# A hybrid decoder trunk: transposing attention weights, queries and keys by DMA, and using them one to two projection groups later

## The chip, the cores and the metric

The kernel runs on one core of a Trainium2 chip. The metric is the device time of one execution in microseconds (us). The engines are TensorE (PE in the profile; PEld is its weight load), VectorE (DVE), ScalarE (ACT), GpSimd (POOL) and SyncE (SP), which here only issues DMAs. Each engine takes its instructions in a fixed order, and an instruction that waits holds up all behind it on its engine.

## The reference, cut to what matters

Two layers (`DEPTH = 2`) over 512 tokens of width 2048. Each layer normalises its input, multiplies it by one wide matrix, feeds three groups of heads, and multiplies their concatenated outputs by a second matrix:

```
proj = rmsnorm(x) @ w_in                 # 512 x 7696
A: y_conv = B * conv3(C * h) * silu(g)   # 512 channels, causal, width 3
B: q, k = rmsnorm per head(q), (k)       # 8 heads of 128, blocks of 128 queries
   z = q k^T / sqrt(128), masked to k < q
   w = exp(log_sigmoid(z) + sum over later keys of log_sigmoid(-z))
   y_sb = (w v) * silu(g)
C: gated linear attention (GLA), 4 heads, chunks of 64, decay exp(cumsum(g))
x = x + concat(y_conv, y_sb, y_gla) @ w_out
```

Weights, inputs and outputs are float32. The kernel keeps that accuracy by splitting an operand into a high and a low fp16 half and adding three products (high x high, high x low, low x high).

## The kernel before, in words

**Projections.** The columns of both matrices are cut into groups of 256: 30 groups of `w_in` and 8 of `w_out` for each layer, 76 in all (`specs`, L261). A group's weights come in two halves of 1 MB. `fetch` (L292) loads a half through SP into a `st` tile (3 buffers); `wmax` (L306) squares it on ACT; `wscale` (L314) takes the maximum over partitions on POOL and makes a power of two on DVE; `whi` (L343, the ACT line is L348) writes the high half `wh`, `wlo` (L351, DVE line L355) the low half `wl` (3 buffers each). `weights` (L368) loads one group ahead. PE uses a group in one of three shapes: `project_cols` (L502, output channels on partitions), `project_toks` (L526, tokens on partitions) and `project_by_token` (L539). Two of the three PSUM banks of pool `psp` hold a group's result.

**Order within a layer.** The GLA inputs come first, then the GLA itself (L666 to L793), then half of the convolution (`conv_in`, `conv_out`), then four attention stages `j` (L856), each of two heads with the groups V, G (gate), Q and K; then the other half of the convolution, then the output projection, group by group (L973). The results of the branches go into the fp16 tiles `mh` and `ml` by `mixsplit` (L580): channel tile 0 to 3 for the convolution, 4 to 11 for attention, 12 to 15 for GLA.

**An attention stage.** V is split into `vh`, `vl`; G becomes the gate `g`. For Q and for K: the squares of each head's row are summed on ACT (L884), a reciprocal root is refined on DVE (`rsqrt`, L189), the rows are scaled into `raw` (L892), PE transposes its eight 128x128 tiles in float32 into PSUM (L900), and ACT and DVE split them into fp16 halves with the K gain as a scale for each partition (L901, L902). Then for each of the two heads and each of two chunks of query tiles (`CHUNKS`, tiles 3 and 2 together, 0 and 1 together): PE makes the scores (L912, L914), ACT and DVE turn them into weights (L918 to L932, with a reversed scan in L928), PE transposes the weights in float32 (L938: seven tiles for the first chunk, three for the second), ACT and DVE split them into `wh`, `wl` (L940, L941), PE multiplies them with V (L946), DVE applies the gate (L949) and `mixsplit` stores.

**What sets the order.** Instructions are emitted in program order and then arranged on each engine by a scheduler with its own timeline; loads of weights have high priority. Where PE's next projection group has room, the scheduler puts transposes, scores and products of attention between its matmuls. The start of the program, up to `order.__exit__` (L496), is written out by hand for DVE and ACT.

**GLA scratch.** The tiles `src16`, `tgt16`, `att16` and `attd` (L137 to L142) have buffers of their own, zeroed once at the start.

Of the kernel before, what the change touches and what calls it, by code (L numbers as in the profile page):

```python
# [5 lines left out]
F32 = mybir.dt.float32  # L6
F16 = mybir.dt.float16
# [10 lines left out]
P = 128  # L18
# [12 lines left out]
CHUNKS = ((((3, 0), (2, 512)), ((0, 0, 256), (1, 256, 256), (2, 512, 256), (3, 768, 128))),  # L31
          (((0, 0), (1, 128)), ((0, 0, 256), (1, 256, 128))))
# [3 lines left out]
def hybrid_trunk(ctx, tc, x, norm_g, w_in, conv_w, conv_b, sb_qn_g, sb_kn_g,  # L36
# [30 lines left out]
    def sm(n, tag, bufs=None):  # L67
        return small.tile([P, n], F32, tag=tag, name=nm(tag), bufs=bufs)
# [64 lines left out]
    avg = const.tile([P, P], F32, tag="avg", name="avg")  # L133
    G.memset(avg, 1.0 / P)
    wup = const.tile([16, depth, 256], F32, tag="wup", name="wup")

    attd = const.tile([P, NT, 2, P], F32, tag="attd", name="attd")  # L137
    att16 = [const.tile([P, NT, 2, P], F16, tag=f"att{i}", name=f"att{i}") for i in range(2)]

    HT = P // 2  # L140
    src16 = [[const.tile([P, seq], F16, tag=f"src{b}{i}", name=f"src{b}{i}") for i in range(2)] for b in range(2)]
    tgt16 = [[const.tile([P, NT, 2, HT], F16, tag=f"tgt{b}{i}", name=f"tgt{b}{i}") for i in range(2)] for b in range(2)]  # L142
    G.memset(attd, 0.0)
# [26 lines left out]
    rows.append((wup, gla_w_up.rearrange("l r c -> r l c")))  # L170
# [32 lines left out]
    kg = const.tile([P, depth], F32, tag="kg", name="kg")  # L203
# [39 lines left out]
    def layer_consts():  # L243
        pps = bank(psm, "m")
        T.transpose(pps[:, :NP], prow, ident[:NP, :NP])
        V.tensor_copy(par, pps[:, :NP])
        for l in range(depth):
            V.tensor_reduce(onmax[:, l:l + 1], pcol("on", l), AX.X, ALU.max, apply_absolute_value=True)
            V.tensor_scalar(onmax[:, l:l + 1], onmax[:, l:l + 1], float(P) ** 0.5, None, ALU.mult)

            gq = sm(2, "kg")
            V.scalar_tensor_tensor(gq[:, 0:1], pcol("qn", l), float(P) ** -0.5, pcol("kn", l), ALU.mult, ALU.mult)
            V.tensor_scalar(gq[:, 1:2], allmax(gq[:, 0:1], 1, "k"), 2.0 ** -20, None, ALU.max)
            pow2(zun[:, l:l + 1], gq[:, 1:2], -20.0, "k")
            V.tensor_scalar(nzun[:, l:l + 1], zun[:, l:l + 1], -1.0, None, ALU.mult)
            V.reciprocal(gq[:, 1:2], zun[:, l:l + 1])
            V.tensor_scalar(kg[:, l:l + 1], gq[:, 0:1], gq[:, 1:2], 2.0 ** -10, ALU.mult, ALU.mult)
            V.tensor_scalar(nbu[:, l, :], par[:, base["bu"] + 2 * l:base["bu"] + 2 * l + 2], -1.0, None, ALU.mult)
# [235 lines left out]
    for a in src16[0] + src16[1] + tgt16[0] + tgt16[1]:  # L494
        V.memset(a, 0.0)
    order.__exit__(None, None, None)  # L496

    for l in range(depth):
# [71 lines left out]
        mh, ml = mix  # L570
        pmix = sm(8, "pmix")
# [36 lines left out]
        V.tensor_scalar(gu[:, 1:2], u, 2.0 ** 35, None, ALU.mult)  # L608
        lrT = wk([LR, seq], "e")
        V.tensor_copy(lrT, tp[:LR, :])  # L610
        Pc = wk([P, 2, seq], "raw", 1)
        for p in range(2):
            gp = bank(psm, "m")
            T.matmul(gp, wup[:, l, p * P:(p + 1) * P], lrT, start=True, stop=True)
# [73 lines left out]
        for p in range(2):  # L688
            Pp, q_, k_ = Pc[:, p, :], gq[:, p, :], gk[:, p, :]

# [84 lines left out]
            for hh in range(2):  # L775
# [7 lines left out]
                T.matmul(ms, avg, sq, start=True, stop=True)  # L783
# [23 lines left out]
        def conv_in(j):  # L807
# [3 lines left out]
            for c in range(2):  # L811
                S.activation(hb[:, c, :], ps[c], AF.Copy, scale=u)
            ps, u = project_cols()
# [4 lines left out]
            for c in range(2):  # L818
# [6 lines left out]
                for d in (1, 2):  # L825
                    V.scalar_tensor_tensor(y[:, c, d:], uc[:, c, :seq - d], w_(2 - d), y[:, c, d:], ALU.mult, ALU.add)  # L826
            return y

        def conv_out(j, y):
# [9 lines left out]

            if j:  # L840
# [15 lines left out]
        for j in range(4):  # L856
# [12 lines left out]
            V.tensor_scalar(vu[:, 0:1], u, 2.0 ** 14, None, ALU.mult)  # L869
            V.tensor_scalar(vu[:, 1:2], u, 1.0, None, ALU.mult)  # L870
            ps, u = project_cols()
            g = gate(ps, u, bm[:, 1:2])
            gm = allmax(bm[:, 0:1], 1, "b")
            m = sm(1, "sbm")
            V.scalar_tensor_tensor(m, gm, vu[:, 0:1], bm[:, 1:2], ALU.mult, ALU.mult)
            s_ = mixscale(2 + j, m, "b")
            qkT = []
            for tag, gain in (("qT", 2.0 ** 10), ("kT", kg[:, l:l + 1])):
                ps, u = project_toks(xh, xl)
                sq = sm(8, "qs")  # L880
                for t in range(NT):
                    for hh in range(2):
                        o = (t % 2) * GW + hh * P
                        S.activation(junk(P), ps[t // 2][:, o:o + P], AF.Square, accum_out=sq[:, 2 * t + hh:2 * t + hh + 1])  # L884
# [5 lines left out]
                raw = wk([P, NT, GW], "raw", 1)  # L890
                for b in range(2):
                    V.tensor_tensor(raw[:, 2 * b:2 * b + 2, :].rearrange("p a (h c) -> p (a h) c", c=P),  # L892
                                    ps[b].rearrange("p (a c) -> p a c", c=P),
                                    rs[:, 4 * b:4 * b + 4].rearrange("p (a o) -> p a o", o=1).to_broadcast([P, 4, P]),
                                    ALU.mult)
                nT_ = wk([P, 2, 2, seq], tag, dt=F16)
                tp = bank2()
                for hh in range(2):
                    for t in range(NT):
                        T.transpose(tp[:, hh, t * P:(t + 1) * P], raw[:, t, hh * P:(hh + 1) * P], ident)  # L900
                S.activation(nT_[:, 0], tp, AF.Copy, scale=gain)  # L901
                V.scalar_tensor_tensor(nT_[:, 1], tp, gain, nT_[:, 0], ALU.mult, ALU.subtract)  # L902
                qkT.append(nT_)
            qT, kT = qkT
            for hh in range(2):
                for qtiles, regs in CHUNKS:
                    q0 = min(t for t, _ in qtiles)
                    zw = sum(n for _, _, n in regs)
                    z = bank2().rearrange("p a c -> p (a c)")
                    for t, o in qtiles:  # L910
                        for i, (a_, b_) in enumerate(((0, 0), (0, 1), (1, 0))):
                            T.matmul(z[:, o:o + (t + 1) * P], qT[:, a_, hh, tsl[t]], kT[:, b_, hh, :(t + 1) * P],  # L912
# [3 lines left out]
                    a = wk([P, zw], "za")  # L916
# [16 lines left out]
                    wT = bank2().rearrange("p a c -> p (a c)")  # L933
                    for kt, ko, n in regs:
                        for t, o in qtiles:
                            if t >= kt:
                                c0 = ko + n - (q0 + 2 - t) * P
                                T.transpose(wT[:, c0:c0 + P], w[:, o + kt * P:o + (kt + 1) * P], ident)  # L938
                    wh, wl = (wk([P, zw], "w" + c, 1, F16) for c in "hl")
                    S.activation(wh, wT[:, :zw], AF.Copy, scale=2.0 ** 14)  # L940
                    V.scalar_tensor_tensor(wl, wT[:, :zw], 2.0 ** 14, wh, ALU.mult, ALU.subtract)  # L941
                    op = bank(psm, "m")[:, :2 * P]
                    hs = slice(hh * P, (hh + 1) * P)
                    for i, (kt, ko, n) in enumerate(regs):
                        for a_, b_ in ((vh, wh), (vh, wl), (vl, wh)):
                            T.matmul(op[:, 2 * P - n:], a_[:, kt, hs], b_[:, ko:ko + n], start=i == 0 and b_ is wh and a_ is vh,  # L946
                                     stop=i == len(regs) - 1 and a_ is vl, skip_group_check=True)
                    y = wk([P, 2 * P], "e")
                    V.scalar_tensor_tensor(y, op, vu[:, 1:2], g[:, hh, q0 * P:(q0 + 2) * P], ALU.mult, ALU.mult)  # L949
                    mixsplit(4 + 2 * j + hh, y, s_, q0)  # L950

        conv_out(1, conv_in(1))
# [20 lines left out]
        for gi in range(NG):  # L973
# [9 lines left out]
            else:  # L983
                ps, u = project_toks(mh, ml, (2, 3) if gi < 2 else ())
# [31 lines left out]
```

## Time and profile before

| What | Value |
|---|---|
| median of 3 runs | 1809.04 us (1807.43 to 1809.38) |
| the profiled execution | 1814.08 us |
| its span, first to last instruction | 1812.3 us |
| granted TensorE clock, mean | 0.996 |
| DMA packets | 180859, 183.74 MB |

The span is that of the one execution from which every row below comes. In a row of grouped instructions, "x160" is their number, then come their busy time in us and the mean ns of one; after the second bar stands the time for which the engine was idle just before them, and what ended it. PE's matmuls overlap in their pipe, so that the time of one is longer than the distance between two. A row of a stretch ("369.80:464.40") gives each engine's busy time in it.

### The profile page before, as it was taken

The page shows a single profiled execution, that of the slowest core. Times are in us where ns is not written, and L with a number is a line of the kernel's source. Part 1 is how long each engine was busy: PE and PEld are TensorE (multiplying, and loading weights), DVE is VectorE, ACT ScalarE, POOL GpSimd, SP SyncE. Part 2 cuts the span into 40 slices and gives each one's busy share as a digit, 9 for nine tenths or more (in the row PEclk, how much of TensorE's full clock was granted, in tenths as well). Part 3 has the DMA queues.
Part 4 walks back from the last instruction along what each step waited for, and adds up shares of the span by engine and source line. Part 5 has one row for each costly group of instructions (what it writes and reads, how often), then busy time and mean ns, then how long its engine had stood idle before and what let it go on. Part 6 is the DMA issues. An engine that isn't in the chain of part 4 may idle for free. (4 is left out here: it accounts for less than half of the span.)

```text
span 1812.3 us, 31149 instructions
## 1 busy us (share of the span) xinstructions
PE 1776.2 (98%) x13164; PEld 1271.9 (70%) x13164; DVE 1046.3 (58%) x1949; ACT 1106.9 (61%) x1671; POOL 43.2 (2%) x98
## 2 busy tenths in 40 slices
PE   7999999999999999999999998999999999999999
PEld 5744456878778764688886454568696878547888
DVE  5456777647464747533464566875655657465432
ACT  8567575567576765555554675675767666665431
POOL 0000000000000000000000000000000000000000
PEclk9999999999999999999999999999999999999999
DMA  6322222232322323354423232222323222224441
GB/s 214 116 93 93 71 93 72 73 113 71 105 83 91 97 74 116 115 182 144 133 81 117 94 93 70 94 82 82 94 91 97 71 94 94 93 94 140 141 139 47
DMA packets 180859, 183.74 MB, mean 101 GB/s; under 512 B 7842, under 2 KB 179948, under 8 KB 180208
## 3 DMA queue, kind: packets, MB, share of 16 engines
q1 hardware_dynamic: 171712, 172.30, 30.2%
q10 hardware_dynamic: 9008, 9.45, 1.6%
q8 instruction: 103, 1.69, 0.4%
q14 instruction: 36, 0.29, 0.1%
HBM read 173.36 MB, written 8.39 MB: 100 GB/s over the span
## 5 line engine op out<-in xcount | busy, mean ns | idle before, releaser
L311 ACT ACTIVATE junk<-st 128x2048 uint8<-128x2048 f32 (+1 forms) x152 | 290.4, 1910 | 290.7 <-DMA st<-in_w_in_dram 203.0
L523 PE MATMUL psp<-wl,m 128*128 128x256 f16 x1664 | 453.5, 273 | 0.0
L522 PE MATMUL psp<-wh,m 128*128 128x256 f16 x1664 | 453.5, 273 | 0.0
L524 PE MATMUL psp<-wh,m 128*128 128x256 f16 x1664 | 453.0, 273 | 0.0
L355 DVE SCALAR_TENSOR_TENSOR wl<-st,ws,wh 128x2048 f16<-128x2048 f32 (+1 forms) x120 | 282.2, 2354 | 118.6 <-ACT wh L348 117.6
L348 ACT ACTIVATE wh<-st,ws 128x2048 f16<-128x2048 f32 (+1 forms) x120 | 239.4, 1996 | 64.1 <-PE psp L524 40.8
L522 PE MATMUL psp<-wh,x 128*128 128x256 f16 x768 | 209.3, 273 | 0.0
L523 PE MATMUL psp<-wl,x 128*128 128x256 f16 x768 | 209.3, 273 | 0.0
L524 PE MATMUL psp<-wh,x 128*128 128x256 f16 x768 | 208.8, 273 | 0.0
L514 PE MATMUL psp<-x,wh 128*128 128x512 f16 x512 | 194.9, 381 | 1.0 <-ACT qT L648 1.0
L515 PE MATMUL psp<-x,wh 128*128 128x512 f16 x512 | 194.8, 381 | 0.0
L516 PE MATMUL psp<-x,wl 128*128 128x512 f16 x512 | 194.4, 381 | 0.0
L514 PE MATMUL psp<-m,wh 128*128 128x512 f16 x512 | 194.1, 379 | 0.0
L515 PE MATMUL psp<-m,wh 128*128 128x512 f16 x512 | 194.0, 379 | 0.0
L516 PE MATMUL psp<-m,wl 128*128 128x512 f16 x512 | 193.2, 379 | 0.0
L516 PEld LDWEIGHTS <-wl 128*128 128x128 f16 x1024 | 100.3, 98 | 120.5 <-issue 4.7
L514 PEld LDWEIGHTS <-wh 128*128 128x128 f16 x1024 | 100.3, 98 | 118.7 <-issue 4.8
L515 PEld LDWEIGHTS <-wh 128*128 128x128 f16 x1024 | 100.4, 98 | 118.2 <-issue 5.6
L524 PEld LDWEIGHTS <-m 128*128 128x128 f16 x1664 | 162.8, 98 | 20.2 <-issue 1.7
L523 PEld LDWEIGHTS <-m 128*128 128x128 f16 x1664 | 162.9, 98 | 20.1 <-issue 1.0
L522 PEld LDWEIGHTS <-m 128*128 128x128 f16 x1664 | 162.9, 98 | 19.6 <-issue 0.3
L321 DVE TENSOR_SCALAR wq<-wgm 128x1 f32<-128x1 f32 x76 | 16.2, 213 | 250.3 <-POOL wgm L318 249.3
(270 smaller groups left out, 2425.9 us busy)
## 6 DMA issues: line engine op xcount, KB each, us to landing
st<-in_w_in_dram SPq DMA_DIRECT2D x120, 1024.0 KB, 5.3
st<-in_w_out_dram SPq DMA_DIRECT2D x32, 1024.0 KB, 5.8
x<-in_x_dram SPq DMA_DIRECT2D x4, 1024.0 KB
qT<-in_x_dram ACTq DMA_DIRECT2D x8, 512.0 KB, 4.0
qT<-xs ACTq DMA_DIRECT2D x8, 512.0 KB, 3.7
xs<-x SPq DMA_DIRECT2D x14, 256.0 KB, 2.5
out_dram<-kT SPq DMA_DIRECT2D x14, 256.0 KB, 2.1
g<-in_norm_g_dram ACTq DMA_DIRECT2D x2, 512.0 KB
```

The costliest lines, as they stand in the source:

```text
L311: S.activation(junk(HK * n).rearrange("p (k n) -> p k n", k=HK), staged[i][h][:, :, :n], AF.Square, accum_out=peak[i][:, h:h + 1])
L321: V.tensor_scalar(m, gm[:, 0:1], gm[:, 1:2], 2.0 ** -120, ALU.add, ALU.max)
L348: S.activation(wh[:, ks, :n], staged[i][h][:, ks, :n], AF.Copy, scale=s_)
L355: V.scalar_tensor_tensor(wl[:, ks, :n], staged[i][h][:, ks, :n], s_, wh[:, ks, :n], ALU.mult, ALU.subtract)
L514: T.matmul(o, wh[:, kk, cs], xh[:, :, k, :], start=st_, stop=False)
L515: T.matmul(o, wh[:, kk, cs], xl[:, :, k, :], start=False, stop=False)
L516: T.matmul(o, wl[:, kk, cs], xh[:, :, k, :], start=False, stop=en)
L522: T.matmul(o, ah[:, t, k, :], wh[:, kk, :n], start=st_, stop=False, skip_group_check=True)
L523: T.matmul(o, ah[:, t, k, :], wl[:, kk, :n], start=False, stop=False, skip_group_check=True)
L524: T.matmul(o, al[:, t, k, :], wh[:, kk, :n], start=False, stop=en, skip_group_check=True)
```

## The change

- `CHUNKS` keeps the places of the query tiles and drops the columns of the transposed weights.
- Q and K (L878 to L903): the square's output goes into `raw` and no longer into a scrap tile; `raw` for K is made by eight products of 128x128 that include the gain, now a full row `kg[:, l, :]` on all partitions (made once for each layer by one more matmul); ACT and DVE split `raw` from SBUF into a new tile `qp` (one buffer), and two DMAs from SP (`dma_start_transpose`, high and low) transpose its eight tiles into `qT` or `kT`.
- Attention weights: they are split before they are transposed, in the memory of `a`; four DMAs for each head (high and low of the two chunks) write the transposed tiles into a new tile `th`. PE's transposes in L900 and L938 are gone.
- Order: `attend` puts four closures into a list: the scores of head 0, of head 1, the products with V of head 0, of head 1. `go()` runs the next one. In the next stage the scores of head 0 come after group V, those of head 1 after G, the products of head 0 after Q and of head 1 after K; for the last stage the groups of the second convolution half stand in, and the products of head 1 come just before the output projection, whose first two groups take channel tile 11 late.
- GLA scratch: `src16` and `tgt16` are views of `mh`, `att16` of `ml`, in channel tiles 4 to 11, zeroed by POOL in each layer; `attd` is a work tile zeroed twice in each layer. The DVE memsets of the start are gone. `avg` is one column, read with a step of zero. The GLA up-projection `wup` is loaded by SP in each layer into a work tile.

The core of the diff:

```
-            for tag, gain in (("qT", 2.0 ** 10), ("kT", kg[:, l:l + 1])):
+            for gain in (None, kg[:, l, :]):
...
-                        S.activation(junk(P), ps[t // 2][:, o:o + P], AF.Square, accum_out=sq[:, 2 * t + hh:2 * t + hh + 1])
+                        S.activation(raw[:, t, hh * P:(hh + 1) * P], ps[t // 2][:, o:o + P], AF.Square,
+                                     accum_out=sq[:, 2 * t + hh:2 * t + hh + 1])
...
-                        T.transpose(tp[:, hh, t * P:(t + 1) * P], raw[:, t, hh * P:(hh + 1) * P], ident)
-                S.activation(nT_[:, 0], tp, AF.Copy, scale=gain)
-                V.scalar_tensor_tensor(nT_[:, 1], tp, gain, nT_[:, 0], ALU.mult, ALU.subtract)
+                            V.scalar_tensor_tensor(raw[:, t, hh * P:(hh + 1) * P], ps[t // 2][:, o:o + P],
+                                                   rs[:, 2 * t + hh:2 * t + hh + 1], gain, ALU.mult, ALU.mult)
...
+                parts = wk([P, 2, NT * GW], "qp", 1, F16)
+                S.activation(parts[:, 0], raw.rearrange("p t c -> p (t c)"), AF.Copy, scale=top)
+                V.scalar_tensor_tensor(parts[:, 1], raw.rearrange("p t c -> p (t c)"), top, parts[:, 0],
+                                       ALU.mult, ALU.subtract)
...
+                for i in range(2):
+                    nc.sync.dma_start_transpose(nT_[:, i].rearrange("p t h c -> p (t h) c"), parts[:, i])
...
-                                T.transpose(wT[:, c0:c0 + P], w[:, o + kt * P:o + (kt + 1) * P], ident)
-                    wh, wl = (wk([P, zw], "w" + c, 1, F16) for c in "hl")
-                    S.activation(wh, wT[:, :zw], AF.Copy, scale=2.0 ** 14)
-                    V.scalar_tensor_tensor(wl, wT[:, :zw], 2.0 ** 14, wh, ALU.mult, ALU.subtract)
+                    wh, wl = parts[:, :zw], parts[:, 896:896 + zw]
+                    S.activation(wh, w, AF.Copy, scale=2.0 ** 14)
+                    V.scalar_tensor_tensor(wl, w, 2.0 ** 14, wh, ALU.mult, ALU.subtract)
+                    for i, part in enumerate((wh, wl)):
+                        nc.sync.dma_start_transpose(th[hh][:, i, 7 * n:7 * n + zw // P, :], part)
...
+            later.extend((lambda: scores(0), lambda: scores(1), lambda: values(0), lambda: values(1)))
...
+            go()
...
-        conv_out(1, conv_in(1))
+        conv_out(1, conv_in(1, go), go)
+        while later:
+            go()
```

More of the change, by code (lines that the diff above doesn't have):

```diff
@@ L131, in make_masks @@
             V.tensor_scalar(masks[:, li, :], far, float(h), None, ALU.is_equal)
-    avg = const.tile([P, P], F32, tag="avg", name="avg")
+    avg = const.tile([P, 1], F32, tag="avg", name="avg")
     G.memset(avg, 1.0 / P)
-    wup = const.tile([16, depth, 256], F32, tag="wup", name="wup")
-    attd = const.tile([P, NT, 2, P], F32, tag="attd", name="attd")
-    att16 = [const.tile([P, NT, 2, P], F16, tag=f"att{i}", name=f"att{i}") for i in range(2)]
     HT = P // 2
-    src16 = [[const.tile([P, seq], F16, tag=f"src{b}{i}", name=f"src{b}{i}") for i in range(2)] for b in range(2)]
-    tgt16 = [[const.tile([P, NT, 2, HT], F16, tag=f"tgt{b}{i}", name=f"tgt{b}{i}") for i in range(2)] for b in range(2)]
-    G.memset(attd, 0.0)
     def gains(l):
@@ L202, in hybrid_trunk @@
     xun = const.tile([P, depth], F32, tag="xun", name="xun")
-    kg = const.tile([P, depth], F32, tag="kg", name="kg")
+    kg = const.tile([P, depth, P], F32, tag="kg", name="kg")
     zun = const.tile([P, depth], F32, tag="zun", name="zun")
@@ L256, in layer_consts @@
             V.reciprocal(gq[:, 1:2], zun[:, l:l + 1])
-            V.tensor_scalar(kg[:, l:l + 1], gq[:, 0:1], gq[:, 1:2], 2.0 ** -10, ALU.mult, ALU.mult)
+            dg = wk([P, P], "e")
+            V.tensor_scalar(gq[:, 0:1], gq[:, 0:1], gq[:, 1:2], 2.0 ** -10, ALU.mult, ALU.mult)
+            V.tensor_scalar(dg, ident, gq[:, 0:1], None, ALU.mult)
+            T.matmul(pps[:, (l + 1) * P:(l + 2) * P], ones.to_broadcast([P, P]), dg, start=True, stop=True)
+            V.tensor_copy(kg[:, l, :], pps[:, (l + 1) * P:(l + 2) * P])
             V.tensor_scalar(nbu[:, l, :], par[:, base["bu"] + 2 * l:base["bu"] + 2 * l + 2], -1.0, None, ALU.mult)
@@ L570, in hybrid_trunk @@
         mh, ml = mix
+        spare = [[mh[:, t, 4:12, :].rearrange("p k c -> p (k c)")[:, n * seq:(n + 1) * seq] for n in range(2)]
+                 for t in range(NT)]
+        src16, tgt16 = spare[:2], [[a.rearrange("p (t h c) -> p t h c", t=NT, h=2) for a in b] for b in spare[2:]]
+        att16 = [ml[:, t, 4:12, :].rearrange("p k c -> p (k c)").rearrange("p (t h c) -> p t h c", t=NT, h=2)
+                 for t in range(2)]
+        for a in mh, ml:
+            G.memset(a[:, :, 4:12, :], 0.0)
         pmix = sm(8, "pmix")
@@ L608, in hybrid_trunk @@
         V.tensor_scalar(gu[:, 1:2], u, 2.0 ** 35, None, ALU.mult)
+        wup = wk([LR, 2 * P], "ga")
+        nc.sync.dma_start(wup, gla_w_up[l])
         lrT = wk([LR, seq], "e")
@@ L613, in hybrid_trunk @@
             gp = bank(psm, "m")
-            T.matmul(gp, wup[:, l, p * P:(p + 1) * P], lrT, start=True, stop=True)
+            T.matmul(gp, wup[:, p * P:(p + 1) * P], lrT, start=True, stop=True)
             bcol = par[:, base["bu"] + 2 * l + p:base["bu"] + 2 * l + p + 1]
@@ L689, in hybrid_trunk @@
             Pp, q_, k_ = Pc[:, p, :], gq[:, p, :], gk[:, p, :]
+            attd = wk([P, NT, 2, P], "zw")
+            G.memset(attd, 0.0)
             for li, h in enumerate(LEV[:-1]):
@@ L782, in hybrid_trunk @@
                 ms = bank(psm, "m")
-                T.matmul(ms, avg, sq, start=True, stop=True)
+                T.matmul(ms, avg.to_broadcast([P, P]), sq, start=True, stop=True)
                 r_ = wk([P, seq], "e")
@@ L804, in weight_ratio, with conv_in @@
             ratio[l] = (rt_, pmx)
-        def conv_in(j):
+        def conv_in(j, then=lambda: None):
             ps, u = project_cols()
@@ L812, in conv_in @@
                 S.activation(hb[:, c, :], ps[c], AF.Copy, scale=u)
+            then()
             ps, u = project_cols()
@@ L826, in conv_in, with conv_out @@
                     V.scalar_tensor_tensor(y[:, c, d:], uc[:, c, :seq - d], w_(2 - d), y[:, c, d:], ALU.mult, ALU.add)
+            then()
             return y
-        def conv_out(j, y):
+        def conv_out(j, y, then=lambda: None):
             ps, u = project_cols()
@@ L838, in limit @@
                 return m
+            then()
             if j:
@@ L876, in hybrid_trunk @@
             s_ = mixscale(2 + j, m, "b")
+            go()
             qkT = []
-            for tag, gain in (("qT", 2.0 ** 10), ("kT", kg[:, l:l + 1])):
+            for gain in (None, kg[:, l, :]):
                 ps, u = project_toks(xh, xl)
                 sq = sm(8, "qs")
+                raw = wk([P, NT, GW], "raw", 1)
                 for t in range(NT):
@@ L889, in hybrid_trunk @@
                 V.tensor_scalar(rs, rs, u, None, ALU.mult)
[L890 to L896, printed above, removed]
@@ L952, in hybrid_trunk @@
-        conv_out(1, conv_in(1))
+                if gain is None:
+                    for b in range(2):
+                        V.tensor_tensor(raw[:, 2 * b:2 * b + 2, :].rearrange("p a (h c) -> p (a h) c", c=P),
+                                        ps[b].rearrange("p (a c) -> p a c", c=P),
+                                        rs[:, 4 * b:4 * b + 4].rearrange("p (a o) -> p a o", o=1).to_broadcast([P, 4, P]),
+                                        ALU.mult)
+                else:
+                    for t in range(NT):
+                        for hh in range(2):
+                            o = (t % 2) * GW + hh * P
+                            V.scalar_tensor_tensor(raw[:, t, hh * P:(hh + 1) * P], ps[t // 2][:, o:o + P],
+                                                   rs[:, 2 * t + hh:2 * t + hh + 1], gain, ALU.mult, ALU.mult)
```

112 lines of the change are left out of this document (63 added, 49 removed).

## The prediction, made before the result was known

> **What bounds the kernel now.** The first view is the page's head: which engine is full, and where.
>
> ```profile
> span 1812.3 us, 31149 instructions
> PE 1776.2 (98%) x13164; PEld 1271.9 (70%) x13164; DVE 1046.3 (58%) x1949; ACT 1106.9 (61%) x1671; POOL 43.2 (2%) x98
> ...
> PE   7999999999999999999999998999999999999999
> ```
>
> PE is busy in every slice but the first and one in the middle. Busy alone is no proof with pipelined matmuls, so the second view is the attention stages themselves: three whole ones, from V's first matmul to that of the next stage.
>
> ```profile
> core 0: us, PE busy (x) PEld busy (x) DVE busy (x) ACT busy (x) POOL busy (x), PEclk, DMA share, GB/s
> 369.80:464.40 94.60, 94.60 (x778) 75.24 (x777) 57.43 (x93) 63.90 (x102) 2.83 (x5) 1.00 0.30 91
> 464.40:558.90 94.50, 94.50 (x778) 75.27 (x777) 57.43 (x93) 63.90 (x102) 2.79 (x5) 1.00 0.29 90
> 558.90:653.50 94.60, 94.60 (x779) 75.36 (x778) 57.21 (x91) 63.90 (x102) 2.79 (x5) 1.00 0.29 90
> ```
>
> PE is busy for all of each stage, at full clock; ACT is busy for 68% and DVE for 61%. The third view is who PE waited for in attention, in the whole span:
>
> ```profile
> PE psm L946 <- ACT wh L940: 1.4, 2, 0.7
> PE psm L946 <- DVE wl L941: 1.0, 2, 0.5
> PE psz L938 <- ACT zw L932: 0.5, 2, 0.3
> ```
>
> That is 2.9 us in 1812. So in attention every matmul taken from PE shortens the kernel by its place in the stream, as long as nothing makes PE wait instead.
>
> **The change part by part.**
>
> *PE's transposes go.* The groups, by shape, and then two places in PE's timeline that show the distance between two of them:
>
> ```profile
> L938 PE MATMUL psz<-ident,zw 128*128 128x128 f32 x160 | 23.1, 275 | 0.5 <-ACT zw L932 0.5
> L900 PE MATMUL psz<-ident,raw 128*128 128x128 f32 x128 | 19.2, 273 | 0.0
> ```
>
> ```profile
> 408.03 0.93 PE L938 MATMUL psz<-ident,zw 128*128 128x128 f32 x7
> 408.80 0.33 PE L912 MATMUL psz<-kT,qT 128*128 128x128 f16 x3
> ...
> 452.30 0.82 PE L900 MATMUL psz<-ident,raw 128*128 128x128 f32 x6
> 452.95 0.27 PE L523 MATMUL psp<-wl,x 128*128 128x256 f16 x1
> ```
>
> Seven take 408.80 - 408.03 = 0.77 us, six 0.65: 0.109 us each, not the 0.27 of their rows, since they overlap. 160 + 128 = 288 of them are 31.4 us, 3.93 in each of the eight stages. Scores and products with V keep their number and shapes. **-31.4 us.**
>
> *PE gains two matmuls* that spread the K gain, one for each layer, float32, 128x128. Nearest row is L900: between 0.11 and 0.27 each; I take 0.2 each. **+0.4 us**, were they on the path.
>
> *ACT and DVE* do nearly what they did: the splits of 1024, 896 and 384 columns remain, from SBUF instead of PSUM. K's scaling becomes eight products of 128x128 where there were two of 128x512; the nearest row of such a product:
>
> ```profile
> L892 DVE TENSOR_TENSOR raw<-psp,qr 128x512 f32<-128x512 f32 x32 | 20.6, 686 | 0.0
> L745 DVE SCALAR_TENSOR_TENSOR e<-e,kT 128x128 f32<-128x128 f32 x16 | 4.6, 290 | 12.1 <-ACT e L743 12.1
> ```
>
> 8 x 0.29 - 2 x 0.69 = 0.94 us more for DVE in a stage, beside 57.4 of 94.6 busy: hidden, except in the chain below. In 94.6 - 3.9 = 90.7 us, ACT's 63.9 us are 70%; neither engine becomes the bound.
>
> *GLA scratch.* POOL zeroes 4096 fp16 columns twice and 1024 float32 columns twice in each layer.
>
> ```profile
> L143 POOL MEMSET attd<- 128x1024 f32 x1 | 1.0, 955 | 0.0
> L495 DVE MEMSET src<- 128x256 uint32 x4 | 1.1, 272 | 0.0
> ```
>
> At the first row's rate a large one is at most 3.8 us. POOL is busy 2%, and in POOL's new order each large one stands ahead of one weight maximum, which the hand-written start needs soonest; I take 0, with 3.8 us as the bound. DVE loses eight memsets like the second row, 2.2 us, from the start; PE does not wait for them. 0. The `wup` loads (16 KB, two) are ordinary DMAs on SP: 0.
>
> *DMAs transpose.* 96 new issues on SP: 32 of eight tiles (256 KB), 32 of seven, 32 of three: 576 tiles of 32 KB, 18.9 MB, a tenth of what the kernel moves. No transposing DMA is in this trace. The nearest rows:
>
> ```profile
> q1 hardware_dynamic: 171712, 172.30, 30.2%
> ...
> st<-in_w_in_dram SPq DMA_DIRECT2D x120, 1024.0 KB, 5.3
> ...
> out_dram<-kT SPq DMA_DIRECT2D x14, 256.0 KB, 2.1
> ...
> st<-in_w_in_dram SPq DMA_DIRECT2D x4, 64.0 KB, 10.4
> ```
>
> As many bytes in a plain copy land after 2.1 us. The far end is 10.4: 64 KB in short rows, behind a 1 MB load. In between: a packet of 1 KB holds one of 16 engines for 0.302 x 1812.3 x 16 / 171712 = 0.051 us, so that the 1024 packets of a 1 MB load are 3.3 us of its 5.3, and 2.0 are latency. A 256 KB tile read in 256-byte rows (128 fp16) is also 1024 packets. I take that: **3.3 us on the engines and 2.0 of latency**, and keep 2.1 and 10.4 as ends.
>
> Whether PE waits for them is decided by distance. SP, ACT and DVE stay in order, so I follow the built order of the changed program from the end of K's projection, T, with these rows:
>
> ```profile
> L311 ACT ACTIVATE junk<-st 128x2048 uint8<-128x2048 f32 x148 | 282.4, 1908 | 290.6 <-DMA st<-in_w_in_dram 203.0 <-DMA st<-in_w_out_dram 85.4
> L348 ACT ACTIVATE wh<-st,ws 128x2048 f16<-128x2048 f32 x116 | 230.9, 1992 | 62.8 <-PE psp L524 40.8 <-PE psp L515 10.1 <-DVE ws L324 9.2
> L901 ACT ACTIVATE kT<-psz,kg 128x1024 f16<-128x1024 f32 x8 | 8.9, 1114 | 8.6 <-PE psz L900 8.6
> L355 DVE SCALAR_TENSOR_TENSOR wl<-st,ws,wh 128x2048 f16<-128x2048 f32 x116 | 272.3, 2349 | 109.1 <-ACT wh L348 108.1
> L902 DVE SCALAR_TENSOR_TENSOR kT<-psz,kg,kT 128x1024 f16<-128x1024 f32 x8 | 10.2, 1280 | 2.9 <-ACT kT L901 2.9
> ...
> 1788.02 20.97 PE psp L547 x192
> ```
>
> At T the `wh` buffer that K held comes free: ACT writes the next `wh` (to T+2.0), DVE its `wl` (to T+4.4); this frees a `st` buffer, SP issues the second half of the next Q's weights, which land 5.3 us later, T+9.7. ACT's square of that half stands ahead of K's split, so K's high half starts at T+11.7 and ends at T+12.8; by then DVE's scaling (some 2.3 us, ready near T+10.3) is done. DVE's low half ends at T+14.1. Before, the same point came 13.7 us after K: there the last K matmul started at 464.3, and
>
> ```profile
> 464.68 0.28 ACT L884 ACTIVATE junk<-psp 128x128 uint8<-128x128 f32 x1 [3.27 <-PE psp L524]
> ...
> 476.78 1.28 DVE L902 SCALAR_TENSOR_TENSOR kT<-psz,kg,kT 128x1024 f16<-128x1024 f32 x1
> ```
>
> ends at 478.1. SP issues the high half's DMA at T+12.9 and the low half's behind it: 2 x 3.3 + 2.0 puts both in SBUF at T+21.5. PE needs them for the scores after group V (192 matmuls, 20.97 us by the last group's row) and the rest of the products with V of head 1 (12 of 256 and 6 of 128 columns less one, some 1.5): T+22.5. **Hidden, with 1.0 us to spare.** Of the two other places, the products of head 0 come some 43 us after their scores; the first product of head 1 stands ahead of K's second bank, 12.1 us after Q, and its high half is issued about 5.9 us after Q (ACT: the next `wh`, three squares, an exponential, a store, the split itself): 6.2 us for seven tiles, 2.9 + 2.0. Hidden too.
>
> The waits of ACT and DVE themselves hold nothing new: K's squares now wait until Q's `raw` is read, which the row order already has 10 us ahead. On SP, weight loads stand behind transposes that wait for ACT or DVE. The weights have a lead: those of G at 474.51 + 2.35 = 476.9 against their first matmul here,
>
> ```profile
> 487.50 0.38 PE L514 MATMUL psp<-x,wh 128*128 128x512 f16 x1
> ```
>
> 10.6 us. 0, if no transpose waits longer than that.
>
> **Sum:** -31.4 + 0.4 = -31.0 us. Made against the profiled execution's own 1814.08 (span 1812.3 and 1.8 around it) that is 1783.1; that execution is 5.0 above the median of the runs, so against the median 1809.0 it is **1778 us**. 0.2%, about what a measurement of this kernel can tell from no change, is 3.6 us.
>
> **The rivals.**
>
> *Slow transposes (slower).* The place is the scores of head 0, the price twice a DMA's time over the spare: two transposes of x us on the engines and 2.0 latency fit into 9.6 us up to x = 3.8. From there PE waits 2 (x - 3.8) in each of eight stages; what PE saved is eaten at x = 5.8, a landing of 7.8 us. At the far end (landing 10.4, x = 8.4) PE waits 9.2 us in eight stages, 74 us: 1852. The first product of head 1 would then be late too, by 8 x (8.4 x 7/8 + 2.0 - 6.2) = 25 us: 1877. For it speaks that tiles of 128 columns mean short rows and that SP may have to issue each tile's rows by itself, which no row here shows; against it, that only 18.9 MB move and engines are 70% idle.
>
> A page of the Trainium skill speaks against the change: "VectorE: DVE Perf Modes", section "The three transpose paths" and the rules behind it, gives a 128x128 transpose of 16-bit data as 390 ns on TensorE and 1309 ns by DMA, and advises TensorE where PSUM may be the destination. If eight tiles took eight times that, one transposing DMA would be an estimate of 10.5 us and the time 75 to 110 us above the forecast, with or without latency in it. The trace disagrees on TensorE's side: 0.109 us apart here. The page "DMA: Bandwidth & Descriptors", section "Latency and other measured facts", has 261 GB/s for a transposing DMA, 1.0 us as an estimate for 256 KB, by which all would be hidden; no run here shows either.
>
> *Part of the gain lost to the order (faster, less).* PE has no slack of its own: the second bank of V needs K's first bank to be read by T+10.5, and I put that at T+9.2; K's second bank needs Q's banks 12.1 us after Q, put at 10.1. If either is late by 1 to 2 us, or the scores by as much, it costs 8 to 16 us: 1786 to 1794; two of them, up to 1805.
>
> *Weights late behind SP's new waits.* A transpose that waits 15 us instead of 10 would hold a load 5 us: 8 x 5 = 40 us, the whole gain; it needs ACT to fall behind by half a group, which 70% busy does not suggest.
>
> **How the numbers follow.** The forecast, 1772 to 1785 with the two unknown ends of the start and of the added matmuls and up to 0.9 us of wait in a stage: 0.45. Part lost, 1785 to 1805: 0.17. Within 0.2%, 1805 to 1813, where waits just pay for it: 0.05. Slower, by slow transposes (0.28) or late weights (0.05), from 1813 to 1877 and beyond: 0.33, of which about 0.15 lies above 1852. So faster 0.62, same 0.05, slower 0.33, and a range of 1772 to 1852, which leaves out 0.03 below and 0.15 above.
>
> **What would show it.** PE's groups of float32 transposes in attention at zero, its count down by 286, and three stages of some 90.6 us with PE busy for all of each: the main term. The transposing DMAs' row in the DMA issues: a landing under 5.8 us keeps the forecast; above 7.8 the kernel is slower, with PE's scores waiting for a DMA into `kT` or its products for one into `th`. If PE waits for K's or Q's `raw` on DVE, it is the order; if for `wh` or `wl`, SP's queue. The forecast is wrong if the stages do not shorten although PE never waits.

## The result, and the profile after

The changed kernel takes **1812.0 us** (median of 20 runs, 1809.9 to 1818.0) against 1809.1 (20 runs, 1807.4 to 1810.4): a ratio of 1.002, 95% interval 1.0013 to 1.0027. The forecast was 1778. The 31 us of work that TensorE loses are gone from its row, and almost exactly as many us of waiting and of half clock have come in. The head of the page:

```profile
span 1813.3 us, 30857 instructions
PE 1752.1 (97%) x12880; PEld 1242.2 (69%) x12880; DVE 1043.2 (58%) x1993; ACT 1094.1 (60%) x1671; POOL 55.4 (3%) x105
...
PE   7999999999999999899999999999999999998999
```

PE has 284 matmuls fewer and is 24 us less busy, in a span that is 1.0 us longer. The three whole stages that answer to those of before (the columns are those of the prediction's second view):

```profile
369.30:462.80 93.50, 90.78 (x736) 70.69 (x735) 55.77 (x94) 62.49 (x101) 1.99 (x5) 1.00 0.47 116
462.80:555.00 92.20, 91.20 (x744) 71.28 (x742) 57.08 (x99) 62.36 (x103) 1.96 (x5) 1.00 0.46 118
555.00:649.90 94.90, 92.42 (x744) 72.23 (x742) 56.99 (x99) 62.12 (x103) 1.96 (x5) 0.98 0.45 115
```

They were to be 90.6 us long with PE busy throughout. They are 92 to 95, with PE idle for 1.0 to 2.7 us in each, and the last one shows a granted clock of 0.98. Whom PE waited for, in the whole span:

```profile
PE psm L927 <- DVE e L935: 21.9, 9, 8.5
...
PE psp L515 <- DVE raw L981: 1.9, 5, 0.4
...
PE psm L927 <- DMA th<-za: 1.7, 2, 1.4
```

No scores (L883) wait for a DMA into `kT`. What waits is the **second chunk of products with V**: `psm` is one PSUM bank, the second chunk may write it only after DVE has read the first (L935, the gate), and DVE comes to that late. The longest case, at the first output group, on PE and then on DVE:

```profile
743.83 0.27 PE L516 MATMUL psp<-wl,m 128*128 128x256 f16 x1
752.61 1.12 PE L927 MATMUL psm<-th,v 128*128 128x256 f16 x6 [8.51 <-DVE e L935]
753.52 0.42 PE L517 MATMUL psp<-wh,m 128*128 128x256 f16 x1
753.74 0.42 PE L515 MATMUL psp<-wh,m 128*128 128x256 f16 x1
```

```profile
744.59 0.75 DVE L587 SCALAR_TENSOR_TENSOR m<-kT,csmix,m 128x512 f16<-128x512 f32 x1
750.78 0.21 DVE L316 TENSOR_SCALAR wq<-wgm 128x1 f32<-128x1 f32 x1 [5.44 <-POOL wgm L313]
750.91 0.74 DVE L856 SCALAR_TENSOR_TENSOR kT<-psp,wu,kT 128x512 f32<-128x512 f32 x1
...
752.08 0.48 DVE L935 SCALAR_TENSOR_TENSOR e<-psm,vu,g 128x256 f32<-128x256 f32 x1
```

The products of the first chunk were done at 741.2. DVE had nothing to do from 745.3, but the next instruction in its row wants the maximum of the next weights, and L935 stands behind it. That maximum comes from POOL, behind ACT's square, behind a load that SP had issued at 741.2, when DVE had freed a buffer for it (ACT, then POOL):

```profile
748.18 1.91 ACT L306 ACTIVATE junk<-st 128x2048 uint8<-128x2048 f32 x1 [3.62 <-DMA st<-in_w_out_dram]
```

```profile
750.35 0.40 POOL L313 PARTITION_ALL_REDUCE wgm<-wm  x1 [13.73 <-ACT junk L306]
```

PE stands 8.5 us. Then the matmuls are 0.21 us apart instead of 0.109 (753.52 to 753.74), which the stretches show as half the clock:

```profile
741.10:752.50 11.40, 3.00 (x29) 2.54 (x27) 5.79 (x15) 5.10 (x8) 0.40 (x1) 0.81 0.59 185
752.50:758.50 6.00, 5.89 (x30) 4.29 (x30) 4.71 (x10) 3.27 (x6) 0.00 (x0) 0.50 0.17 45
758.50:774.10 15.60, 15.60 (x145) 13.98 (x144) 0.75 (x1) 0.91 (x4) 0.00 (x0) 1.00 0.24 87
```

So this one wait cost 11 us: 8.5, and 2.8 at half clock.

To add it all up I took the distance of each matmul's start to the next and subtracted the usual distance for its form; the sum over a stretch is what PE lost there, by waits or by clock (us, one profile each; the last three columns are experiments below):

| Stretch | before | after | e1 | e9a | e9 |
|---|---|---|---|---|---|
| six inner attention stages | 0.6 | 15.7 | 18.3 | 4.9 | 6.3 |
| first attention stage of each layer | 9.2 | 16.7 | 13.3 | 4.8 | 6.0 |
| second convolution half, both layers | 2.9 | 1.1 | -0.2 | -0.1 | -0.2 |
| first output group, both layers | 1.4 | 18.9 | 0.1 | 18.8 | 0.0 |
| the rest | 33.4 | 26.3 | 29.7 | 30.8 | 30.8 |
| all | 47.5 | 78.7 | 61.2 | 59.2 | 42.9 |
| span less that | 1764.8 | 1734.6 | 1734.9 | 1734.5 | 1734.9 |

The work fell by 30.2 us (forecast: 31.0), the losses rose by 31.2. The last row hardly moves: the same sum gives 1734.5 to 1735.0 us in every profile of a kernel that transposes by DMA, and 1764.8 to 1766.0 where PE transposes. So all that differs between the kernels with transposing DMAs below is what PE loses by waits and by clock.

### The profile page after: what moved, and what is told of

Read it like the earlier page. It is cut to its first block, busy times and chain, and to the rows that moved or that the text cites. A ratio compares the mean times of both kernels' runs of the same rounds, so it can differ in the third digit from the quotient of the medians.

```text
span 1813.3 us, 30857 instructions
## 1 busy us (share of the span) xinstructions
PE 1752.1 (97%) x12880; PEld 1242.2 (69%) x12880; DVE 1043.2 (58%) x1993; ACT 1094.1 (60%) x1671; POOL 55.4 (3%) x105
```

## The experiments

Theory A: the loss is the one bank. B: it is the transposing DMAs. C: it is whatever comes next, as another wait takes the place of the one removed. All times are medians; ratios are against the kernel before on the same chip, with 95% intervals, and the times of different chips are compared by them. Lines of an experiment's own kernel may be shifted against the changed kernel's.

**e1_two_banks.** `op = (bank2()[:, 0, :] if n else bank(psm, "m"))[:, :2 * P]`

> Edit: of the two chunks of products with V, the second writes a psz bank instead of the one psm bank, so that PE need not wait until DVE has read the first chunk (L935). Theory A (one bank, read late by DVE): the 21.9 us of PE waits on DVE L935 go, and with them the stretches at half clock behind three of them (628.8, 752.8 and 1643.4 us: 1.6 + 2.8 + 1.2 us), so 1812.0 - 27.5 = 1784.5 us; 1782 to 1792 with small waits left. Rival B (the transposing DMAs take the time, by landing or by contention): 1808 to 1814. Rival C (another wait takes the place, psz banks or the mix tiles): 1795 to 1808.

1799.7 us, 0.9947 (0.9934 to 0.9961): faster than both kernels. The waits on L935 are gone, the first output group is as short as it can be. But:

```profile
PE psp L515 <- DVE raw L981: 12.6, 6, 3.4
```

This row had 1.9 us. A is right as to the bank and wrong as to the sum, and the time is in C's range: K's second bank now waits until DVE has scaled Q out of the banks.

**e2_early.** `then()` once more, ahead of the last `project_cols()` in `conv_out`.

> Edit: the products of the second head of the last attention stage are written ahead of conv's last projection group instead of behind it; the single psm bank stays. Theory A: only the two waits at the first output group (8.5 and 5.9 us) and the half-clock stretches behind them (2.8 and 1.2) go, 18.4 us; in the new place the second chunk waits as it does in other stages, 0.5 to 2.5 us twice: 1794 to 1799 us. Rival B (DMAs): the products come 11 us of PE work sooner after their DMAs, so PE waits longer for them: 1812 or more. Rival C (what is late there is the weight chain of the output groups, not the order): 1806 to 1812.

1806.7 us, 0.9982 (0.9973 to 0.9991). The output groups no longer wait, yet a 5.6 us wait on L935 with 2.5 us at half clock stands in the convolution group instead. The time is C's, far from A's gain. The profiled execution took 1802.9 us.

**e3_no_later.** After `attend(...)`: `while later: go()`.

> Edit: transposes stay with the DMAs, but scores and products are written right behind K's split as before the change, not one to two groups later. The built order puts the first scores 16.0 us of PE work after K's projection ends (T), where the changed kernel has 21.4; the low half of K is issued at T + 15.3. This measures the landing that no row shows. Theory A (a transposing DMA lands in at most 6.1 us): scores wait 2 to 5.5 us in eight stages, 16 to 44 us, while the two stalls at the output groups (18.4 us) go: 1805 to 1840 us. Rival B (slow DMAs, landing 6 us or a queue behind them): more than 44 us of waits, above 1840. If scores wait under 1 us the deferral was not needed: under 1800.

1815.9 us, 1.0039 (1.0025 to 1.0053): within A's range, but not by A's wait. A had 16 to 44 us of scores waiting for `kT`, and they wait 2.3 us; it is the products that wait for `th`. For L935 nothing waits any more:

```profile
PE psm L927 <- DMA th<-za: 27.9, 18, 3.3
...
PE psz L883 <- DMA kT<-qp: 2.3, 3, 1.5
```

So the later places do hide the DMAs, 30 us of waits (1.7 are left in the changed kernel), and bring others for nearly as much.

**e4_twice.** Each `dma_start_transpose` written twice.

> Edit: every transposing DMA is issued twice, to the same destination: 192 instead of 96, 37.8 MB, twice the time in SP's queue (1.3 us each) and on the engines. Theory A (the DMAs hide, the loss is the bank): the low half of K lands some 3 to 5 us later, T + 24 against scores at T + 21.4, so 0 to 3 us of wait in eight stages: 1812 to 1836, all of it as waits of scores for DMA, none of it on L935. Rival B (DMA time and contention are what ate the gain of 31 us): doubling costs about that again, 1840 or more, spread over projection groups too.

1863.2 us, 1.0296 (1.0281 to 1.0311): outside A's range, where B wanted it. But it doubles more than the DMAs' time: both write one tile, so that SP stands until the first has landed, with the loads of weights behind it:

```profile
SPq L912 <- DMA th<-za: 46.8, 29, 3.3
```

No matmul waits for a transposing DMA. PE waits for the gate again (23.6 us), for K's and Q's scaling (16.1) and for the scales at the output groups (13.7), and 13 stretches at half clock lose 27 us in all. The run doubles SP's issuing, its standing and the traffic at once and does not part them, so it alone does not show that the 96 DMAs cost anything; whether they do is seen in e9.

**e5_k_bank.** On top of e1, K's second bank comes from `psz`.

> Edit: on top of the second chunk of products in psz, the second bank of K's projection is a psz bank too, so that it need not wait until DVE has scaled Q out of its psp banks (L981). In the run with the first edit alone PE waited 12.6 us for that in six stages, and behind two of these waits (636.3 and 1428.2 us) it ran at half clock, 1.6 + 1.6 us lost. Theory A (the loss is PSUM banks read late by DVE, one after the other): 1799.7 - 15.8 = 1783.9 us; 1782 to 1789. Rival C (ACT and DVE are late as a whole, because ACT's row now reaches each weight square as its load lands, so that the next consumer waits instead): 1790 to 1800, with new waits of scores or of products for K, V or the weights.

1841.1 us, 1.0173 (1.0157 to 1.0190): both expectations fail. With the bank free the scheduler put K's squares and split much later into ACT's row (in the six inner stages the DMA is issued 24 to 28 us after K, not 13), and scores wait 39.3 us. This order hides what the bank alone would be worth. It also gives the landing that had no row (SP, then PE):

```profile
587.10 2.61 SPq L999 DMA_TRANSPOSE kT<-qp  x2
```

```profile
590.52 0.58 PE L883 MATMUL psz<-kT,qT 128*128 128x512 f16 x1 [7.01 <-DMA kT<-qp]
```

256 KB transposed (the high half, the first of the two issues): 3.4 us from issue to use.

**e6_gla_only.** The kernel before with the GLA scratch part alone.

> Edit: the kernel before with the GLA scratch part alone (zeroed spare channel tiles for the sources, targets and attention of GLA, attd and wup in work tiles, avg of one column); attention and its transposes as before. The forecast put this part at 0, with 3.8 us as the bound: 1805 to 1813 us. By the stages of the two traces the GLA part of the changed kernel is 7 us shorter (3.2 and 3.0 in the GLA groups) and the first attention stages have 7.5 us more waits: if both come from the GLA part, 1808 to 1811; if only the gain does, 1801 to 1804; if only the loss, 1814 to 1818.

1808.7 us, 0.9991 (0.9982 to 1.0000): the part is worth nothing, as forecast.

**e7_pe_later.** The later places, with TensorE's transposes.

> Edit: the changed kernel with TensorE's transposes back (288 of 128x128, float32, 31.4 us) and the later places of scores and products kept: the order alone, without transposing DMAs. Theory A (the later places bring the waits, whoever transposes): the waits on the single psm bank stay, 1812 + 31 = 1843 us; 1828 to 1850, as psz is now shared with transposes. Rival B (the DMAs ate the gain): without them the order costs nothing, so the time is that of before, 1805 to 1813.

1829.1 us, 1.0100 (1.0086 to 1.0114). The later places cost 18 us here, with PE working as long as before the change and no transposing DMA; B's range is missed. A's time is at best at its edge (by the ratio, 1827 us), and its wait is not there: none on the gate, PE's transposes wait for the exponential instead:

```profile
PE psz L908 <- ACT zw L904: 13.0, 11, 2.1
```

**b_again.**

> The kernel before, once more with a profile: how far one profiled execution of one kernel stands from another. Every theory expects 1807 to 1815 us, with PE's waits in attention within 1 us of the first profile's 2.9; the number of stretches at half clock (four, 5.9 us in the first profile) tells how much of such a difference is the clock.

1809.9 us; span 1808.1 against 1812.3, with two stretches at half clock (3.1 us lost) instead of four (5.9). One profile is good to about 4 us.

Theory D (ACT, standing at weight squares, is what makes the others late) came from ACT's waits in the three stages (before, then after):

```profile
ACT junk L311 <- DMA st<-in_w_in_dram: 28.8, 6, 5.9
```

```profile
ACT junk L306 <- DMA st<-in_w_in_dram: 46.9, 17, 8.1
```

ACT now stands 17 times instead of 6 for a load of weights that it is about to square, with Q's squares and the softmax queued behind.

**e8_no_prio.** On top of e1, `load_(i)` without `tc.high_priority()`.

> Edit: on top of the second chunk of products in psz, the loads of weights (square, maximum, high and low half) lose the scheduler's high priority, so that where both are ready, ACT and DVE do Q's and K's squares and splits first. In the run with the first edit alone ACT's row reached each weight square a median 5.2 us after its load was issued, as it landed (10.5 in the kernel before), and stood still for it. Theory D (ACT stands at weight squares, and so Q's squares, DVE's scaling and PE's second bank of K are late): the 12.6 us of waits on Q's scaling shrink to 0 to 8 us, 1785 to 1797. Theory A (the banks alone): no change, 1798 to 1802, as the squares stay where they are among the loads. If the weights become late instead, PE waits for them and it is above 1802.

1811.4 us, 0.9977 (0.9968 to 0.9985): worse than e1 and in neither theory's range; it is above 1802, but it is not the weights that PE waits for. The squares stay where they were in ACT's row, and 14.3 us of waits for the split of the attention weights on DVE (its line L905) take the place of Q's.

**e9_no_square** and **e9a_no_square**, the same in the changed kernel: the 60 squares of 30 groups of weights, with their 30 maxima and scales, are left out.

> Edit: on top of the second chunk of products in psz, the weights of 15 of the 16 projection groups in the attention stages of a layer are left without a square, maximum and scale of their own, and take the scale of the first; that leaves out part of the computation (60 of 152 squares, 1.9 us each on ACT, their maxima on POOL and five small operations on DVE). PE's work stays. Theory D (ACT standing at weight squares for loads makes Q's scaling late): PE's waits in the attention stages go, and what PE saved shows: 1799.7 - 17.7 = 1782 us; 1779 to 1788. Theory A (a bank that is read late because of the order, with or without squares): 1792 to 1800, with the waits on Q's scaling still above 6 us.

> Edit: the same omission of 60 squares, maxima and scales in the changed kernel itself, with the single psm bank. Theory D: products in the attention stages no longer wait for DVE, as it is not behind a standing ACT; only the first output group keeps its two waits (8.5 and 5.9 us, there for weights of w_out, and 4.0 us at half clock behind them): 1812 - 15 = 1797 us; 1793 to 1801. Theory A: the waits on the single bank stay in the stages too, 0.5 to 2.5 us each: 1803 to 1812.

1780.5 us, 0.9814 (0.9801 to 0.9827), and 1795.5 us, 0.9897 (0.9883 to 0.9910): both far from A and where D wants them. (The kernel before was 0.3% slower on this chip; by the ratios they are 1775 and 1790 us on the first, some 3 us below D's ranges.) In the table above the two edits add up: the second bank takes away the loss of the first output groups (18.9 to 0.1), the omitted squares most of that in the attention stages (15.7 + 16.7 to 4.9 + 4.8), and e9 has both. Stages of the forecast are there now:

```profile
365.70:456.30 90.60, 90.60 (x743) 71.33 (x741) 52.67 (x74) 48.38 (x85) 0.40 (x1) 1.00 0.49 129
456.30:546.90 90.60, 90.60 (x744) 71.33 (x742) 54.11 (x80) 47.77 (x87) 0.36 (x1) 1.00 0.48 120
```

90.6 us, PE busy in all of it, with all 96 transposing DMAs in place: in such a stage they cost PE nothing, and theory B is out. ACT has 48 us of work in a stage where it had 62.

**e10_four_st.** On top of e1, a fourth buffer for loads.

> Edit: on top of the second chunk of products in psz, a fourth buffer for weights on their way in (256 columns each; the 16 gate columns of GLA go to small tiles of their own), so that a load is issued one half, some 11 us, sooner and lies in SBUF when ACT's row reaches its square; all is computed. Theory D (ACT stands at weight squares for loads that have just been issued; leaving 60 squares out gave 1780.5 us): ACT no longer stands in the attention stages, PE's waits there go, 1782 to 1788 us, stages of 90.6 us. If the scheduler only moves the squares one half earlier and ACT stands at them as before: 1795 to 1802.

1802.3 us, 0.9957 (0.9944 to 0.9971): not better than e1. ACT stands less (35.4 us for loads in three stages; e1: 50.5), and Q's scaling is as late as ever (16.0 us of waits). Less standing did not mend the bank, so D in its first form, the standing alone, is not borne out.

**e11_q_first** and **e12_q_first_four.** `with tc.high_priority():` around squares, root and scaling of Q and K, on top of e1 and of e10.

> Edit: on top of the second chunk of products in psz, the squares, root and scaling of Q and K get the scheduler's high priority, as the loads of weights have it; all is computed. In the built rows of ACT, Q's last squares move ahead of the next high half of weights (2.0 us), the root ahead of the second split of the weights (0.5 us) and Q's split ahead of a weight square (1.9 us). Theory D1 (the place of Q's work in ACT's row, not the loads themselves, makes the bank late): the six waits on Q's scaling, 12.6 us with 3.1 us at half clock behind two of them, lose about 2.5 us each and go: 1799.7 - 14 = 1786 us; 1782 to 1792. Theory D2 (ACT stands for loads at the squares that stay ahead): 1796 to 1803.

> Edit: the same priority for Q's and K's squares, root and scaling on top of the kernel with the fourth load buffer (1802.3 us); all is computed. That kernel had ACT standing 25 us less at weight squares in the attention stages than with three buffers, and still 16.0 us of waits on Q's scaling in six stages, with half-clock stretches behind them. Theory D1: the waits lose 2 to 3 us each and nearly go, 1784 to 1791 us. Theory D2 (standing for loads): the two edits help together, 1780 to 1786, where the priority alone gives 1796 or more.

1807.8 us, 0.9991 (0.9983 to 1.0000), and 1802.0 us, 0.9961 (0.9948 to 0.9975): no gain over e1 and e10, and neither D1 nor D2 has its times. In e12 Q's scaling is waited for more (20.8 us). In e11 the waits move on once more, from Q's scaling to the transposed attention weights:

```profile
PE psm L927 <- DMA th<-za: 11.0, 6, 2.9
PE psp L515 <- DVE raw L982: 5.6, 8, 0.9
```

**e13_square_only** (squares taken, sums unused, maxima and scales left out as in e9) and **e14_short_square** (each over 256 columns).

> Edit: as in the kernel without the 60 squares (scale of the first group, second chunk of products in psz), but the 60 squares are taken all the same and their sums not used; left out are only the maximum on POOL and the small scale operations on DVE. Theory D1' (ACT's row is what is late: 1.9 us of square each and the standing for the load ahead of it): as if nothing were left out, 1795 to 1802 us against 1799.7 with all and 1780.5 without the squares. Rival E (the way of the scale over POOL and DVE holds DVE's row): 1779 to 1787.

> Edit: as the kernel that takes the 60 squares and does not use them, but each over 256 columns instead of 2048 (0.4 us instead of 1.9 on ACT): ACT's row still comes to each load and stands there until it has landed, but the work is gone. If the standing is what makes Q's scaling late: 1792 to 1800 us. If the 1.9 us of work are: 1779 to 1787. In between, both.

1802.9 us, 0.9963 (0.9947 to 0.9980), and 1789.6 us, 0.9889 (0.9871 to 0.9906). The squares on ACT, of e13 and then e14:

```profile
L306 ACT ACTIVATE junk<-st 128x2048 uint8<-128x2048 f32 x148 | 282.9, 1912 | 318.2 <-DMA st<-in_w_in_dram 224.9 <-DMA st<-in_w_out_dram 92.0
```

```profile
L307 ACT ACTIVATE junk<-st 128x256 uint8<-128x256 f32 x60 | 25.0, 417 | 104.7 <-DMA st<-in_w_in_dram 104.5
```

The way over POOL and DVE is worth nothing (0.9963 against e1's 0.9947). Of the 0.0149 between e13 and e9, half, 0.0074 or 13 us, goes with 60 x 1.5 = 90 us of ACT's work: ACT stands for loads as long in e14 as in e13 (38.6 and 36.9 us in the three stages). The other half, 0.0075 or 14 us, goes with the standing (9.1 us in e9) and the remaining 25 us of work. Both count. Q's scaling is still waited for in e14, 12.6 us (17.2 in e13, 3.8 in e9), and the halves are rough, since the scheduler arranged some instructions otherwise in each of the three.

## Why the prediction was wrong, point by point

- **PE's transposes: right.** -31.0 forecast, -30.2 found; a stage of 90.6 us exists, in e9.
- **GLA scratch: right**, 0 (e6).
- **The DMAs: right in the chain, too dear in price.** Between the end of K and its scores, on PE, SP and PE again:

```profile
553.87 0.27 PE L517 MATMUL psp<-wh,x 128*128 128x256 f16 x1
```

```profile
566.80 2.61 SPq L999 DMA_TRANSPOSE kT<-qp  x2
```

```profile
576.48 0.81 PE L883 MATMUL psz<-kT,qT 128*128 128x512 f16 x3
```

T is 554.0: the high half goes out at T + 12.8 (12.9 forecast), the scores start at T + 22.5 (22.5), and do not wait. The landing is 3.4 us alone (5.3 forecast) and 5.4 as the median of those into `th`:

```profile
th<-za SPq DMA_TRANSPOSE x64, 5.4
```

The rival of slow transposes is out. The Trainium skill ("VectorE: DVE Perf Modes", section "The three transpose paths") gives 1309 ns for a tile by DMA; the 10.5 us for eight that the prediction estimated from it are three times the 3.4 us measured here. What a transposing DMA costs beyond it is SP's own time:

```profile
L999 SPq DMA_TRANSPOSE qT<-qp x16: 1232/1274/2841, 363.0 to 1537.6; - x16
```

a median of 1.27 us to issue one, where a load of weights takes 0.37 (the median of L295).

- **The step that failed** is "ACT's 63.9 us are 70%; neither engine becomes the bound", and with it the sum's 0 for PE's waits on ACT and DVE. By busy time neither is the bound. But ACT and DVE run in order, and a stage is a loop through both, with PE's banks at each end: scores, softmax, split; Q, squares, root, scaling; load, square, maximum, high half, low half. What was priced at nothing came to 31.2 us: 15.1 more in the six inner stages, 17.5 at the first output groups, the rest nearly even. The wait comes out at whichever bank or tile is read or written last: the gate's L935 in the changed kernel, Q's scaling in e1, the split of the attention weights in e8, their transposes in e11. With all work done and the later places kept, no edit gave more than e1; e9, e9a and e14, which take work off ACT, gave, by the ratios, 24, 22 and 10 us more than the kernel each began from (e1, the changed kernel, e1). Two things can use up the slack, a PE stage 4 us shorter and the later places; e7 shows that the places alone cost 18 us at the old length, and no run has the shorter stage without them and without waits for DMAs.
- **"The products of head 0 come some 43 us after their scores"** and so "hidden too": that looked at the landing of `th` alone, and not at who reads the bank that the products write. The rival "part of the gain lost to the order" had the right kind of cause, but it named V's and K's banks, not `psm`, and allowed 8 to 16 us for one; the output groups alone took 17.5.
- **Half clock behind a wait** was no term of the sum. It was in the trace of before already, four times.
- **The chances.** "Waits just pay for it" had 0.05. The range held the time only by luck, because slow transposes had stretched it; of the 34 us between forecast and time, waits for transposing DMAs are 1.7.

What stays open: each kernel here has its own built order, so that some us between any two may be the order's. How much of the 31 us a better order of ACT's row would give back with all work done, no run shows; e1, by its second bank, gives 13 of them.

## What to carry to other kernels

An engine at 100% gives way only as far as the in-order rows that feed and drain it: before work is taken off it, follow, for the new length of the loop, each PSUM bank to its reader and list what stands ahead of that reader in its row. Busy shares of 60 to 70% did not show it here. And when the wait changes its name with each repair, look for work to take off the row instead of moving the wait: here leaving out squares worked, as an experiment and not as a repair, since the kernel needs their scales.

## What the runs showed of the hardware that was not expected

- TensorE's granted clock drops to 0.50 in or behind some of its waits, in stretches of 3.4, 6.8 or 10.2 us, and costs 1.1 to 2.8 us on top of the wait (the 8.5 us wait above: 2.8). In the 18 profiles here, after the first 60 us, all 21 waits of PE over 3.5 us have such a stretch, 44 of 65 between 2.0 and 3.5 us, and 13 of 81 between 1.4 and 2.0. The longest without one is 3.4 us, in e1 at 447 us.
- Transposing 18.9 MB added 76,816 packets, of 246 bytes each, and 118 us of all 16 engines' time (the queue's share, against 30.2% before):

```profile
q1 hardware_dynamic: 248528, 191.19, 36.7%
```

that is 1891 / 76816 = 0.025 us of one engine for a packet, half of what the forecast took over from plain loads.
